# The weight ring's upper and lower tiles begin at eight offsets past a multiple of 64 bytes

## The chip, the cores and the metric

The kernel runs on one core of one Trainium2 chip. The metric is the device time of one execution in microseconds (us), as the median of several runs; the profile is one further execution, recorded by the hardware profiler. TensorE (PE) multiplies, VectorE (DVE) and ScalarE (ACT) work elementwise, GpSimd (POOL) helps, and SyncE (SP) issues the DMAs that bring the weights from HBM into SBUF, the on-chip memory of 128 partitions.

## What is computed

A trunk of two layers on 256 rows of 2,048 features. Each layer is a mixing block (retention in layer 0, mLSTM in layer 1) and an MLP, each with an RMSNorm ahead and behind. Nearly all the time goes into the products with the weights:

```python
def retention(h, w_in, w_out, cos, sin):
    q, k, v, g = split(h @ w_in)            # 2048 x 12288
    ...
    return (silu(g) * y) @ w_out            # 4096 x 2048

def mlstm(h, w_in, b_gate, norm_g, w_out):
    q, k, v, o, gates = split(h @ w_in)     # 2048 x 6160
    ...
    return (y * sigmoid(o)) @ w_out         # 2048 x 2048

def sqrelu_mlp(h, w1, w2):                  # 2048 x 8192, 8192 x 2048
    return square(relu(h @ w1)) @ w2

def reference(x, ...):
    for i in range(2):
        h = rms_norm(x, g[0])
        y = retention(h, ...) if i % 2 == 0 else mlstm(h, ...)
        x = x + rms_norm(y, g[1])
        y = sqrelu_mlp(rms_norm(x, g[2]), w1[i], w2[i])
        x = x + rms_norm(y, g[3])
    return x
```

## The kernel before

**Numbers in two parts.** TensorE multiplies in the type float32r, which keeps fewer bits than float32. So each operand is split into an upper part (rounded to float32r) and a lower part (the rest), and a product is made of three: upper by upper, upper by lower, lower by upper. The activations lie split in `hT` (all 2,048 features, upper and lower parts side by side) and in `zT` (one slice of 512).

**The ring.** The weights come in 899 loads of 128 x 1,024 float32 (`CE` = 1024 columns, 4,096 bytes in a partition). SP loads each into a tile `raw` (four of them in turn). ACT rounds `raw` into a tile `wh`, the upper part (L935), and DVE writes `wl = raw - wh`, the lower part (L954; in the first loads of a few blocks half of it falls to GpSimd, L953). `wh` and `wl` have nine tiles each (`SPLIT`), in the pool `wp`, used in turn. All tiles of a pool that have one tag lie behind each other, so that with slots of 4,096 bytes every tile of the ring has the same address modulo 64. The small tile `spare` ahead of them (224 bytes in a partition) moves the ring's start: in the built program `raw` begins at 86,720, `wh` at 103,104 and `wl` at 139,968, all multiples of 64, as `hT` (50,368) and both `zT` (176,832 and 185,024) are.

**Two forms of product.** In `mm_a` the weights stream through the array (the moving operand, 512 columns) and a 128 x 128 piece of the activations is held (the stationary operand). A load serves 12 matmuls: for each half of 128 rows of tokens, and for each of the two runs of 512 columns in the tile,

```python
nc.tensor.matmul(ps, xh, wh[:, i, cols], ...)   # L133
nc.tensor.matmul(ps, xh, wl[:, i, cols], ...)   # L134
nc.tensor.matmul(ps, xl, wh[:, i, cols], ...)   # L135
```

In `mm_b` it is the other way round: a 128 x 128 piece of the weights is held, and `hT` streams: 512 columns (upper and lower activations together) over a piece of `wh` (L145, or L148 at the end of a sum), then 256 columns (upper activations) over the same piece of `wl` (L146). A load serves eight such pairs. `mm_a` is used for v, g and o, for all products out of a block, and for the first 512 columns of each MLP; `mm_b` for q, k and the rest of the first MLP product.

**The attention's own product.** `mm_pv` (L317 to L319) has the pattern of `mm_a`: upper scores by `vh`, upper scores by `vl`, lower scores by `vh`. `vh` and `vl` are tiles of 1,032 float32, or 4,128 bytes, which is 64 times 64.5. `vh` begins at a multiple of 64; `vl`, which lies right behind, begins 32 bytes past one. In the retention layer a matmul takes 512 columns of them. In the mLSTM layer it takes 258 columns, at steps of 1,032 bytes, so that its starts are 0, 8, 16 or 24 bytes (`vh`) and 32, 40, 48 or 56 bytes (`vl`) past a multiple of 64. The scores' own tiles begin at multiples of 64.

**The order of the work** is written out by hand (`tc.manual_schedule()`): a list of steps is walked, and ahead of each step as many loads are split as the ring has room for (`gone + SPLIT`, and `pace(n)` at the start). No instruction is put elsewhere by a scheduler.

Of the kernel before, what the change touches and what calls it, by code (L numbers as in the profile page):

```python
# [10 lines left out]
F32 = mybir.dt.float32  # L11
F32R = mybir.dt.float32r
# [7 lines left out]
P = 128  # L20
# [10 lines left out]
CE = KA * 512  # L31
# [29 lines left out]
def trunk(ctx, tc, x, xt, positions, gcols, grows, w_rqk, w_rvg, w_ro, w_mqk, w_mvo, w_mg, b_gate,  # L61
# [3 lines left out]
    gap = ctx.enter_context(tc.tile_pool(name="gap", bufs=1))  # L65
    wp = ctx.enter_context(tc.tile_pool(name="wp", bufs=SPLIT))
# [5 lines left out]

    gc_sb = const.tile([P, 2, 4, KT], F32, name="gc_sb")
    nc.gpsimd.dma_start(out=gc_sb.rearrange("p a b k -> p (a b k)"), in_=gcols)
    spare = gap.tile([P, 56], F32, name="spare")
    nc.gpsimd.memset(spare, 0.0)
    ident = const.tile([P, P], F32, name="ident")
    make_identity(nc, ident)
# [42 lines left out]
    def later(delay, fn):  # L121
        due.append((now[0] + delay, fn))
# [772 lines left out]
    def pace(n):  # L895
        return (n + 1) // 2 if n < 16 else int(8 + (n - 15) * PACE)
# [9 lines left out]
    def load_to(end):  # L906
        for i in range(loaded[0], min(end, len(loads))):
            before = {1: (2, 4), 2: (4, 8), 4: (8, 12), 6: (12, 16)}
            if i in before:
                load_xt(*before[i])  # L910
            for k in range(XN * (i - X0), XN * (i - X0 + 1)):
                if 0 <= k < 8:
                    load_x(k // 4, k % 4)
            tiles[i] = wp.tile([P, CE], F32, tag="raw", name="raw", bufs=RAW)
            if i == 0:
                nc.sync.dma_start(out=tiles[i][:, 0:512], in_=w_rvg[0, 0, :, 0:512])
                load_xt(0, 2)
                nc.sync.dma_start(out=tiles[i][:, 512:CE], in_=w_rvg[0, 0, :, 512:CE])
            else:
                loads[i](tiles[i])  # L920
            loaded[0] = i + 1

    ctx.enter_context(tc.manual_schedule())
    load_to(1)
    warm_up()
    for n, (ids, fn) in enumerate(steps):
        now[0] = n
        while gone < len(loads) and last_use[gone] < n:
            gone += 1
        while split < len(loads) and split < min(gone + SPLIT, pace(n)):  # L930
            load_to(split + RAW)
            raw = tiles[split]
            wh = wp.tile([P, CE], F32R, tag="wh", name="wh")
            for part in (slice(0, 512), slice(512, CE)) if split == 0 else (slice(0, CE),):
                nc.scalar.copy(wh[:, part], raw[:, part])  # L935
            packed = split in packed_ids
            wl = wh if packed else wp.tile([P, CE], F32R, tag="wl", name="wl")
            tiles[split] = (wh, wl)

            def low_packed(wh=wh, raw=raw):  # L940
                h, r = (t.rearrange("p (t c) -> p t c", c=P) for t in (wh, raw))
                nc.vector.tensor_tensor(h[:, :, 64:104], r[:, :, 0:40], h[:, :, 0:40].bitcast(F32),
                                        op=ALU.subtract)

            def low(easy=split in easy_ids, wh=wh, wl=wl, raw=raw):
                h = wh.bitcast(F32)
                cut = CE // 2 if easy else CE
                if n == 1:
                    for part in (slice(0, 512), slice(512, CE)):
                        nc.vector.tensor_tensor(wl[:, part], raw[:, part], h[:, part], op=ALU.subtract)  # L950
                    return
                if easy:
                    nc.gpsimd.tensor_tensor(wl[:, cut:CE], raw[:, cut:CE], h[:, cut:CE], op=ALU.subtract)  # L953
                nc.vector.tensor_tensor(wl[:, 0:cut], raw[:, 0:cut], h[:, 0:cut], op=ALU.subtract)  # L954
            if packed:
                later(0, low_packed)
            elif split in ids or n < 2:
                low()
            else:
                later(0, low)  # L960
            split += 1
        fn([tiles[i] for i in ids])
        for d in [d for d in due if d[0] <= n]:
            due.remove(d)
            d[1]()
# [79 lines left out]
```

## Time and profile before

| | us |
|---|---|
| median of 3 runs | 2580.02 (2579.06 to 2583.42) |
| the profiled execution | 2580.38 |
| its span, first to last instruction | 2578.7 |
| TensorE busy | 2552.2 (99%) |
| VectorE busy | 1653.5 (64%) |
| ScalarE busy | 1199.4 (47%) |
| mean granted TensorE clock | 0.998 of full speed |

A matmul's duration in the profile is modelled and reaches past the start of the next one, since matmuls are pipelined. How fast TensorE works is therefore read from the starts: the distance from one matmul's start to the next one's. The timeline gives starts to 0.01 us, so a distance is taken over many matmuls and divided by their number.

### The profile page before, as it was taken

The numbers are of one execution on the slowest core, as the hardware profiler recorded it, in microseconds if no ns is written. First come the engines' busy times: TensorE is split into PE (matmuls) and PEld (weight loads), VectorE is DVE, ScalarE is ACT, GpSimd is POOL, SyncE is SP. The second block draws the span as 40 slices with busy tenths as digits, with TensorE's granted clock in tenths as the row PEclk, the third lists the DMA queues.
The fourth block names the chain that finished last, engine by engine and source line by source line (L and its number), as shares of the span: only waits on it lengthen the run. The fifth ranks groups of instructions, "written<-read, shape, count | busy, mean of one in ns | idle before, by whom it ended". The sixth has DMA issues, their size and how long they took to land.

```text
span 2578.7 us, 33319 instructions
## 1 busy us (share of the span) xinstructions
PE 2552.2 (99%) x12629; PEld 2152.9 (83%) x12629; DVE 1653.5 (64%) x2147; ACT 1199.4 (47%) x1602; POOL 227.0 (9%) x253
## 2 busy tenths in 40 slices
PE   8999999999999999999999999999999999999998
PEld 7888888888878888888888788888788888888887
DVE  8755665665675666656666766555866656666665
ACT  7444444444455444444444565545564444444443
POOL 1200110110130000000000210000300000000002
PEclk9999999999999999999999999999999999999999
DMA  8555555555546565655555556555465655555553
GB/s 298 195 182 195 189 171 200 184 181 182 189 141 212 186 200 175 202 184 196 181 195 180 180 191 207 176 203 186 143 218 173 197 192 191 180 199 184 189 202 124
DMA packets 135153, 486.85 MB, mean 189 GB/s; under 512 B 15368, under 2 KB 15392, under 8 KB 134992
## 3 DMA queue, kind: packets, MB, share of 16 engines
q1 hardware_dynamic: 131904, 476.11, 55.0%
q0 software_dynamic: 2512, 7.56, 1.3%
q8 instruction: 99, 1.62, 0.2%
q10 hardware_dynamic: 576, 1.05, 0.1%
q14 instruction: 62, 0.51, 0.1%
HBM read 482.55 MB, written 2.11 MB: 188 GB/s over the span
## 4 chain that ended last, share of the span: by engine, by line
PE 93%; DVE 3%; DMA 1%; issue 1%; ACT 1%; POOL 0%; DVEq 0%; ACTq 0%; POOLq 0%
PE acc L145 22%; PE acc L134 18%; PE acc L135 18%; PE acc L133 18%; PE acc L146 12%; PE acc L148 1%; DVE wl L954 1%; DMA raw<-w_mqk 1%; PE tr L397 1%; DVE hT L410 1%; DVE x_sb L358 0%; PE sc L527 0%; DMA raw<-w_mvo 0%; DVE yacc L271 0%; PE pv L319 0%
## 5 line engine op out<-in xcount | busy, mean ns | idle before, releaser
L935 ACT CAST wh<-raw 128x1024 fp32r<-128x1024 f32 (+1 forms) x899 | 936.6, 1050 | 999.7 <-PE acc L135 584.1
L954 DVE TENSOR_TENSOR wl<-raw,wh 128x1024 fp32r<-128x1024 f32 x895 | 1078.3, 1237 | 288.4 <-ACT wh L935 287.6
L145 PE MATMUL acc<-hT,wh 128*128 128x512 f32 x2520 | 894.3, 398 | 0.0
L146 PE MATMUL acc<-hT,wl 128*128 128x256 f32 x2688 | 741.3, 281 | 0.0
L145 PEld LDWEIGHTS acc<-hT,wh 128*128 128x128 f32 x2520 | 473.4, 188 | 113.7
L133 PE MATMUL acc<-wh,zT 128*128 128x512 f32 (+1 forms) x1424 | 552.2, 388 | 0.0
L135 PE MATMUL acc<-wh,zT 128*128 128x512 f32 (+1 forms) x1424 | 551.1, 387 | 0.0
L134 PE MATMUL acc<-wl,zT 128*128 128x512 f32 (+1 forms) x1424 | 550.9, 387 | 0.0
L146 PEld LDWEIGHTS acc<-hT,wl 128*128 128x128 f32 x2688 | 507.7, 189 | 7.3
L133 PE MATMUL acc<-wh,hT 128*128 128x512 f32 x828 | 326.4, 394 | 0.0
L134 PE MATMUL acc<-wl,hT 128*128 128x512 f32 x828 | 323.6, 391 | 0.4 <-DVE wl L954 0.4
L135 PE MATMUL acc<-wh,hT 128*128 128x512 f32 x828 | 323.4, 391 | 0.0
L134 PEld LDWEIGHTS acc<-wl,zT 128*128 128x128 f32 x1424 | 267.4, 188 | 54.4
L135 PEld LDWEIGHTS acc<-wh,zT 128*128 128x128 f32 x1424 | 267.3, 188 | 54.4
L133 PEld LDWEIGHTS acc<-wh,zT 128*128 128x128 f32 x1424 | 267.4, 188 | 53.1
L240 DVE TENSOR_TENSOR yacc<-acc,yacc 128x512 f32<-128x512 f32 x288 | 195.7, 690 | 164.6 <-PE acc L135 162.2
L134 PEld LDWEIGHTS acc<-wl,hT 128*128 128x128 f32 x828 | 156.1, 189 | 33.0 <-DVE wl L954 1.5
L135 PEld LDWEIGHTS acc<-wh,hT 128*128 128x128 f32 x828 | 156.0, 188 | 32.7
L133 PEld LDWEIGHTS acc<-wh,hT 128*128 128x128 f32 x828 | 156.1, 188 | 31.4
L153 DVE TENSOR_TENSOR r<-acc,r 128x256 f32<-128x256 f32 x120 | 50.5, 421 | 196.1 <-ACT r L152 196.1
L869 POOL TENSOR_TENSOR r<-r 128x512 f32<-128x512 f32 x60 | 62.5, 1041 | 1229.0 <-DVE r L867 1229.0
L872 DVE TENSOR_TENSOR zT<-r,zT 128x512 fp32r<-128x512 f32 x60 | 41.6, 693 | 73.3 <-POOL r L869 73.3
(189 smaller groups left out, 1084.3 us busy)
## 6 DMA issues: line engine op xcount, KB each, us to landing
raw<-w SPq DMA_DIRECT2D x256, 512.0 KB, 4.2
raw<-w1b SPq DMA_DIRECT2D x240, 512.0 KB, 4.5
raw<-w_rvg SPq DMA_DIRECT2D x127, 512.0 KB, 4.2
raw<-w_rqk SPq DMA_DIRECT2D x64, 512.0 KB, 4.1
raw<-w_ro SPq DMA_DIRECT2D x64, 512.0 KB, 4.2
raw<-w_mvo SPq DMA_DIRECT2D x64, 512.0 KB, 4.2
raw<-w_mqk SPq DMA_DIRECT2D x32, 512.0 KB, 4.3
raw<-w_mo SPq DMA_DIRECT2D x32, 512.0 KB, 4.3
```

Of the source, the lines that this page charges most:

```text
L133: nc.tensor.matmul(ps, xh, wh[:, i, cols], start=first and i == 0, stop=False)
L134: nc.tensor.matmul(ps, xh, wl[:, i, cols], start=False, stop=False)
L135: nc.tensor.matmul(ps, xl, wh[:, i, cols], start=False, stop=last and i == KA - 1)
L145: nc.tensor.matmul(ps[j], wh[:, i, sl], xt[:, kt0 + i, :], start=first and i == 0, stop=False)
L146: nc.tensor.matmul(ps[j][:, 0:S], wl[:, i, sl], xt[:, kt0 + i, 0:S], start=False, stop=False)
L148: nc.tensor.matmul(ps[j], wh[:, i, sl], xt[:, kt0 + i, :], start=False, stop=True)
L153: nc.vector.tensor_tensor(dst, ps[:, 0:S], dst, op=ALU.add)
L240: nc.vector.tensor_tensor(dst, box[t], dst, op=ALU.add)
L869: nc.gpsimd.tensor_tensor(r2, r, r, op=ALU.mult)
L872: nc.vector.tensor_tensor(mids[s][:, 2 * half:2 * half + 2, S:2 * S], r2, h.bitcast(F32), op=ALU.subtract)
L935: nc.scalar.copy(wh[:, part], raw[:, part])
L954: nc.vector.tensor_tensor(wl[:, 0:cut], raw[:, 0:cut], h[:, 0:cut], op=ALU.subtract)
```

## The change

The tiles of `wh` and `wl` get 16 columns more (slots of 4,160 bytes, 65 times 64, so that every slot still begins at a multiple of 64), and of each only 1,024 columns are used, which begin 2k columns, or 8k bytes, into the slot. For load number i, k is i mod 8 for `wh` and (i + i // 8) mod 8 for `wl`. So from load to load the starts go up by 8 bytes and come round after eight, and the difference between `wl` and `wh` of the same load is 8 x (i // 8 mod 8) bytes: none for eight loads, 8 bytes for the next eight, and so on. `spare` becomes 64 bytes smaller (224 to 160), which moves `raw` and the ring down by 64.

```diff
-    spare = gap.tile([P, 56], F32, name="spare")
+    spare = gap.tile([P, 40], F32, name="spare")
...
+    def shifted(k, nm):
+
+        room = wp.tile([P, CE + 16], F32R, tag=nm, name=nm)
+        return room[:, 2 * k:2 * k + CE]
+
...
-            wh = wp.tile([P, CE], F32R, tag="wh", name="wh")
+            wh = shifted(split % 8, "wh")
...
-            wl = wh if packed else wp.tile([P, CE], F32R, tag="wl", name="wl")
+            wl = wh if packed else shifted((split + split // 8) % 8, "wl")
```

Every engine's instructions stand in the same order as before, with the same shapes; only addresses differ. In the built program `raw` begins at 86,656, the slots of `wh` at 103,040 and of `wl` at 140,480; what lies behind the ring (`zT`, `vh`, `vl` and the other work tiles) moves up by 1,088 bytes, 17 times 64, and so keeps its offset past a multiple of 64; `hT` stays.

Counted over the built program, `mm_a` has 6,660 matmuls of 512 columns. In 5,424 of them the load's `wl` and `wh` have different offsets, in 1,236 the same; 820 of the 6,660 have a moving operand that begins at a multiple of 64 (before: all). `mm_b` has 2,688 pairs, with the eight offsets about equally often for either held part.

## Rows read from the trace of the kernel before

**Rows 1.** The page: span; busy time, share of span and instructions of engines.
```profile
span 2578.7 us, 33319 instructions
...
PE 2552.2 (99%) x12629; PEld 2152.9 (83%) x12629; DVE 1653.5 (64%) x2147; ACT 1199.4 (47%) x1602; POOL 227.0 (9%) x253
...
PEclk9999999999999999999999999999999999999999
```

**Rows 2.** What TensorE waited for: total us, times, longest us.
```profile
PE tr L397 <- DVE x_sb L358: 10.0, 6, 3.0
PE acc L177 <- DVE hT L581: 6.7, 1, 6.7
PE acc L134 <- DVE wl L954: 0.4, 1, 0.4
```

**Rows 3.** Groups by line and shape: count, busy us, mean ns, idle before.
```profile
L145 PE MATMUL acc<-hT,wh 128*128 128x512 f32 x2520 | 894.3, 398 | 0.0
L146 PE MATMUL acc<-hT,wl 128*128 128x256 f32 x2688 | 741.3, 281 | 0.0
L133 PE MATMUL acc<-wh,zT 128*128 128x512 f32 x1392 | 542.7, 390 | 0.0
...
L133 PE MATMUL acc<-wh,hT 128*128 128x512 f32 x828 | 326.4, 394 | 0.0
...
L148 PE MATMUL acc<-hT,wh 128*128 128x512 f32 x168 | 62.9, 396 | 0.0
```

**Rows 4.** Timeline of PE, a long run of mm_a: start us, duration, instruction.
```profile
846.65 0.39 PE L133 MATMUL acc<-wh,zT 128*128 128x512 f32 x1
...
848.26 0.39 PE L134 MATMUL acc<-wl,zT 128*128 128x512 f32 x1
...
868.21 0.39 PE L135 MATMUL acc<-wh,zT 128*128 128x512 f32 x1
```

**Rows 5.** Timeline of PE around the last retention head's mm_pv.
```profile
706.83 0.39 PE L135 MATMUL acc<-wh,zT 128*128 128x512 f32 x1
...
709.10 0.39 PE L317 MATMUL pv<-vh,pth 128*128 128x512 f32 x1
709.33 0.40 PE L318 MATMUL pv<-vl,pth 128*128 128x512 f32 x1
709.56 0.39 PE L319 MATMUL pv<-vh,ptl 128*128 128x512 f32 x1
...
711.19 0.39 PE L133 MATMUL acc<-wh,zT 128*128 128x512 f32 x1
```

**Rows 6.** Timeline of PE: mm_b under way, then where mm_b begins.
```profile
842.40 0.40 PE L145 MATMUL acc<-hT,wh 128*128 128x512 f32 x1
842.64 0.28 PE L146 MATMUL acc<-hT,wl 128*128 128x256 f32 x1
...
845.58 0.40 PE L145 MATMUL acc<-hT,wh 128*128 128x512 f32 x1
...
868.43 0.39 PE L145 MATMUL acc<-hT,wh 128*128 128x512 f32 x1
868.66 0.28 PE L146 MATMUL acc<-hT,wl 128*128 128x256 f32 x1
868.77 0.40 PE L145 MATMUL acc<-hT,wh 128*128 128x512 f32 x1
...
869.12 0.40 PE L145 MATMUL acc<-hT,wh 128*128 128x512 f32 x1
869.37 0.28 PE L146 MATMUL acc<-hT,wl 128*128 128x256 f32 x1
869.49 0.40 PE L145 MATMUL acc<-hT,wh 128*128 128x512 f32 x1
```

**Rows 7.** Timeline of PE: mm_a on 256 columns.
```profile
747.13 0.28 PE L134 MATMUL acc<-wl,zT 128*128 128x256 f32 x1
...
749.03 0.29 PE L135 MATMUL acc<-wh,zT 128*128 128x256 f32 x1
```

**Rows 8.** Timeline of PE: mLSTM's mm_pv, 18 matmuls, and the next one.
```profile
1652.86 0.28 PE L317 MATMUL pv<-vh,pth 128*128 128x258 f32 x1
...
1655.02 0.40 PE L145 MATMUL acc<-hT,wh 128*128 128x512 f32 x1
```

**Rows 9.** Groups of ACT and DVE that write the ring.
```profile
L954 DVE TENSOR_TENSOR wl<-raw,wh 128x1024 fp32r<-128x1024 f32 x883 | 1064.4, 1238 | 288.4 <-ACT wh L935 287.6
L935 ACT CAST wh<-raw 128x1024 fp32r<-128x1024 f32 x897 | 935.4, 1051 | 995.5 <-PE acc L135 584.1 <-PE acc L145 260.9 <-issue 60.2
```

## The prediction

> **What bounds the kernel now.** The page comes first: TensorE is busy for 2552.2 of the 2578.7 us of the span, at a full granted clock (2.4 GHz), and no other engine comes near (VectorE 64%, ScalarE 47%) [rows 1]. The waits say the same: TensorE waited for a part of the ring only once, for 0.4 us, and for anything else for some 17 us in all [rows 2]. So the time is the number of matmuls times the distance from one start to the next, and a change that alters neither the order nor the shapes can only act through that distance (or by slowing another engine until TensorE waits for it). The groups give the numbers [rows 3]: 2,688 pairs of `mm_b` (2,520 of L145 and 168 of L148, each with one L146), and 3 x (1,392 + 828) = 6,660 matmuls of `mm_a` with 512 columns. The timeline gives the distances. In a long run of `mm_a`, from 848.26 to 868.21 us, 88 distances take 19.95 us, or 0.2267 us each [rows 4]. In `mm_b`, nine pairs from 842.40 to 845.58 take 3.18 us, or 0.3533 us a pair [rows 6]. 6,660 x 0.2267 + 2,688 x 0.3533 = 1,510 + 950 = 2,460 us, 95% of the span: one nanosecond in the distance of `mm_a` is 6.7 us, one in the pair of `mm_b` 2.7 us.
>
> **A distance that isn't one number.** The same form of matmul doesn't always take 0.2267 us. Where `mm_a` begins after `mm_b`, its first seven distances, from 846.65 to 848.26, take 1.61 us, or 0.230 each, and only then is the pace 0.2267 [rows 4]. And `mm_pv` of the retention layer, which has the pattern of `mm_a` and the same 512 columns, is slower though it starts out of the settled pace: ten distances before it take 2.27 us (0.227 each), its first `vh` still 0.23, but the eight from the first `vl` on, 709.33 to 711.19, take 1.86 us, or 0.2325 each [rows 5]. What sets it apart from `mm_a` is that `vl` begins 32 bytes past a multiple of 64 and `vh` at one, so that the moving operand's offset changes twice in three matmuls. That is what the change brings to `mm_a`. I read the rows so: matmuls that follow each other with equal offsets fall into step and reach 0.2267; those whose offsets differ don't, and take up to 0.2325.
>
> **The change part by part.**
>
> *`mm_a` with different offsets, 5,424 of the 6,660.* The bounds: 0 if they stay in step, and 0.2325 - 0.2267 = 5.8 ns if they behave as `mm_pv`. A gain isn't excluded by arithmetic, since 512 columns at the granted 2.4 GHz are 213.3 ns and 13.4 ns are left to gain (6,660 x 13.4 = 89 us), but no stretch in the rows runs below 0.2267. The row to which they are nearest is `mm_pv`: same pattern, same number of columns. Its offsets differ by half of 64 bytes, though, and here a fifth of the 5,424 have differences as small as 8 bytes (or 56, which is 8 from the other side), and for those I expect less. So I take 4.5 ns: 5,424 x 4.5 ns = 24.4 us.
>
> *`mm_a` with equal offsets, 1,236.* Within a load nothing alternates, but from one load to the next, after 12 matmuls, the start moves by 8 bytes. If that costs one settling, as after `mm_b`, it is 7 x 3.3 ns = 23 ns a load, or 1.9 ns a matmul: 1,236 x 1.9 ns = 2.4 us. The bounds are 0 and, if they never settle, 5.8 ns, 7.2 us.
>
> *`mm_b`, 2,688 pairs.* The moving operand stays where it was; the held pieces, 128 columns of `wh` and `wl`, now begin at the eight offsets. No row shows a held operand off a multiple of 64. The bounds from the nearest rows: where `mm_b` begins out of the settled pace its first pair takes 0.34, the next 0.35, then 0.37 [rows 6]; so it has an in-step pace of its own, 0.34, that it loses after a pair. If the offsets let it keep that, the gain is 13 ns x 2,688 = 36 us; if each pair were as long as the slowest start distances near there (0.24 for the 512 columns, 0.12 for the 256), 0.36, the loss is 7 ns x 2,688 = 18 us. I take 0: the pairs are out of step already, and another offset is as likely to shorten the one distance as to lengthen the other.
>
> *Matmuls of 256 columns.* The 96 of `mm_a` on 256 columns run at 1.90 / 16 = 0.119 us with equal offsets [rows 7], and the mLSTM layer's 258 columns, with offsets from 0 to 56 bytes, at 2.16 / 18 = 0.120 [rows 8]. Short matmuls don't show a price of the offset; 0 is taken. It also says that the start's offset alone is cheap, and that it is the settled pace of the 512 that is at stake.
>
> *The writers of the ring.* ACT and DVE now write at offsets of 8k bytes, and DVE reads `wh` there. DVE has some 883 such instructions of 1.24 us and ACT 897 of 1.05 [rows 9]; DVE is idle for 925 us of the span, so each of its 883 could take 1.0 us longer before it had no time left. The cover is the ring's nine tiles and TensorE's 99%. I take 0. The loads into `raw` keep their offsets, and so do `hT`, `zT` and the work tiles.
>
> *Sum.* 24.4 + 2.4 = 26.8 us on the profiled execution's 2580.38, which is its span of 2578.7 and 1.7 around it: 2607.2. The median of the runs is 0.4 us lower, 2580.02, so 2607 there, 1.0% slower.
>
> **A rule that says otherwise.** In the rows an alternation of 0 and 32 bytes goes with 0.2325 for 0.2267 [rows 5]. The Trainium skill (SBUF — State Buffer, Specifications) states that SBUF has cachelines of 16 bytes, and that each step to a new line pays. By that rule 2,048 bytes that begin 8 bytes off a line touch 129 lines in place of 128; an estimate from the page and the row is 0.2267 / 128 = 1.8 ns for the half of the matmuls with such a start, 3,330 x 1.8 ns = 6 us, or nothing at all where the extra line is hidden. 32 bytes are two whole lines, so by it `vl` should run as `vh` does, and the trace doesn't agree.
>
> **The rivals.**
>
> *No change.* The start's offset costs nothing, and `mm_pv` is slow for another reason: its runs are only nine long, it writes to other accumulators (`psB`), and its held tiles are others. For it: the short matmuls, which run at any offset at the same pace [rows 7, 8]. Against it: `mm_pv` comes out of the settled pace, and leaves it at the very first `vl`, after a `vh` of 0.23 [rows 5]. Time: 2580, or up to 2585 where only each load's first matmuls resettle, one or two of twelve. Chance 0.14.
>
> *`mm_b` falls into step: faster.* Its pair goes from 0.3533 towards the 0.34 of its first pair [rows 6], because the held pieces no longer begin where the moving operand does. The price is up to -36 us, against +27 of `mm_a`; it decides the sign once `mm_b` keeps step for three quarters of its pairs, or for a third if `mm_a` loses only the 12 us of half the price. With all pairs in step and `mm_a` at half price: 2580 - 36 + 13 = 2557; with two thirds of the pairs: 2569. For it: the state exists in the rows. Against it: it lasts one pair there, and the eight offsets would have to serve it nearly all. Chance 0.16.
>
> *The change doesn't do what it says.* The slots' starts are multiples of 64 in the built program, and all tiles but the ring's keep their offsets, so the shifts are real. No chance is set aside.
>
> **How the numbers follow.** My forecast, `mm_a` out of step, has 0.70. Its own range runs from half the price in `mm_a` with `mm_b` unchanged, 2580 + 13 = 2593, to the full price with the loss in `mm_b`: 5,424 x 5.8 + 2.4 + 18 = 52 us, 2632. The range that is to hold 8 times in 10 takes in the rival of no change and the lesser gains in `mm_b` below it, down to 2574, and ends above at 2630; what is left out is most of the faster case and a little at the top. About 0.2%, 5 us, is what a measurement of this kernel can tell from no change. Slower by more than that: the forecast, 0.70. Within it: 0.14. Faster: 0.16.
>
> **What would show it.** In the timeline after: a long run of `mm_a` whose load has different offsets at 0.230 to 0.2325 a start, beside one with equal offsets near 0.2267; pairs of `mm_b` at 0.353; the same waits of TensorE as before. In the groups the 512-column matmuls of L133 to L135 (now some lines lower) keep their number. Wrong would be: `mm_a` at 0.2267 throughout (then the reading of `mm_pv` falls), `mm_b` at 0.34 or at 0.36 (then the held operand's offset counts, and my 0 was the error), or waits of TensorE for `wl` (then DVE pays for the offsets).

## The result and the profile after

The changed kernel takes 2605.66 us (2605.57 to 2606.89) against 2580.02: 1.0098 times as long, with an interval of 1.0075 to 1.0121. That is 25.6 us more, where 26.8 were forecast. The page of the changed kernel (span; busy time and share by engine), which answers to [rows 1]:

```profile
span 2603.9 us, 33319 instructions
...
PE 2579.9 (99%) x12629; PEld 2155.3 (83%) x12629; DVE 1652.7 (63%) x2147; ACT 1196.9 (46%) x1602; POOL 225.9 (9%) x253
```

VectorE and ScalarE are as busy as before to within 3 us, so the writers of the ring pay nothing for the offsets; the 25 us of the span are all TensorE's. What TensorE waited for (total us, times, longest us), as in [rows 2]:

```profile
PE tr L397 <- DVE x_sb L358: 7.8, 6, 2.5
PE acc L177 <- DVE hT L581: 6.4, 1, 6.4
PE acc L134 <- DVE wl L959: 0.8, 2, 0.4
```

There is no new wait. The loss is in the starts. Timeline of PE after the change, the settled part of a run of `mm_a` (its eighth to its last matmul) and the run of `mm_b` behind it, to be read as [rows 4] and [rows 6]:

```profile
904.45 0.39 PE L134 MATMUL acc<-wl,zT 128*128 128x512 f32 x1
...
924.86 0.40 PE L135 MATMUL acc<-wh,zT 128*128 128x512 f32 x1
...
926.48 0.39 PE L145 MATMUL acc<-hT,wh 128*128 128x512 f32 x1
...
943.59 0.40 PE L145 MATMUL acc<-hT,wh 128*128 128x512 f32 x1
```

The 88 distances of `mm_a` take 20.41 us, 0.2319 each (before: 0.2267), and the 49 pairs of `mm_b` take 17.11 us, 0.3492 each (before: 0.3533).

Over the whole trace, from all starts but those behind a wait (a distance of over 0.262 us): `mm_a` goes from a mean of 227.0 to 232.6 ns, and 6,602 x 5.54 ns = +36.6 us; `mm_b`'s pair from 352.7 to 349.9 ns, and 2,672 x -2.84 ns = -7.6 us. What the starts behind waits take beyond the mean distance of their kind of matmul goes from 24.1 to 21.1 us. 36.6 - 7.6 - 3.0 = 26.0, against 25.6 measured.

### The profile page after: what moved, and what is told of

The parts are those of the page before. It is cut to its first block, busy times and chain, and to the rows that moved or that the text cites. A ratio compares the mean times of both kernels' runs of the same rounds, so it can differ in the third digit from the quotient of the medians.

```text
span 2603.9 us, 33319 instructions
## 1 busy us (share of the span) xinstructions
PE 2579.9 (99%) x12629; PEld 2155.3 (83%) x12629; DVE 1652.7 (63%) x2147; ACT 1196.9 (46%) x1602; POOL 225.9 (9%) x253
## 4 chain that ended last, share of the span: by engine, by line
PE 92%; DVE 4%; DMA 1%; issue 1%; ACT 1%; POOL 1%; DVEq 0%; ACTq 0%; POOLq 0%
PE acc L145 21%; PE acc L134 19%; PE acc L133 19%; PE acc L135 19%; PE acc L146 11%; DVE wl L959 2%; PE acc L148 1%; PE tr L397 1%; DVE hT L410 1%; DMA raw<-w_mqk 1%; DVE x_sb L358 1%; PE sc L527 0%; DVE yacc L271 0%; DMA raw<-w_mvo 0%; PE pv L319 0%
## 5 line engine op out<-in xcount | busy, mean ns | idle before, releaser
L959 DVE TENSOR_TENSOR wl<-raw,wh 128x1024 fp32r<-128x1024 f32 x895 | 1078.3, 1236 | 298.0 <-ACT wh L940 296.3
L133 PE MATMUL acc<-wh,zT 128*128 128x512 f32 (+1 forms) x1424 | 560.1, 393 | 0.0
L134 PE MATMUL acc<-wl,zT 128*128 128x512 f32 (+1 forms) x1424 | 558.2, 392 | 0.0
L135 PE MATMUL acc<-wh,zT 128*128 128x512 f32 (+1 forms) x1424 | 558.0, 392 | 0.0
L133 PE MATMUL acc<-wh,hT 128*128 128x512 f32 x828 | 330.2, 399 | 0.0
L134 PE MATMUL acc<-wl,hT 128*128 128x512 f32 x828 | 327.1, 395 | 0.8 <-DVE wl L959 0.8
L135 PE MATMUL acc<-wh,hT 128*128 128x512 f32 x828 | 327.1, 395 | 0.0
L134 PEld LDWEIGHTS acc<-wl,zT 128*128 128x128 f32 x1424 | 268.7, 189 | 60.9
L135 PEld LDWEIGHTS acc<-wh,zT 128*128 128x128 f32 x1424 | 268.0, 188 | 61.5
L134 PEld LDWEIGHTS acc<-wl,hT 128*128 128x128 f32 x828 | 156.6, 189 | 36.7 <-DVE wl L959 1.6
L135 PEld LDWEIGHTS acc<-wh,hT 128*128 128x128 f32 x828 | 156.2, 189 | 36.6
```

Of the source, the lines that this page charges most:

```text
L133: nc.tensor.matmul(ps, xh, wh[:, i, cols], start=first and i == 0, stop=False)
L134: nc.tensor.matmul(ps, xh, wl[:, i, cols], start=False, stop=False)
L135: nc.tensor.matmul(ps, xl, wh[:, i, cols], start=False, stop=last and i == KA - 1)
```

## The experiments

In all of them instructions, shapes and order stay those of the kernel before, unless the diff says otherwise; only starts of tiles differ. The diffs are shortened: a value or a comment stands where the run's kernel calls a small function. Times stand beside runs of the kernel before on the same chip (2580.6 to 2581.6). "Relative start" is the start of a ring tile less that of the activations that it is multiplied with. Modulo 256 `hT` and `zT` begin alike in the kernel before and in all runs with slots of a multiple of 256 bytes. In the changed kernel and the runs built on it (slots of 4,160 bytes, the smaller `spare`) `zT`, which lies behind the ring, is 1,088 bytes further up, or 64 modulo 256, while `hT` stays.

### One constant offset, nothing alternates modulo 64

```diff
-            wh = shifted(split % 8, "wh")
+            wh = shifted(1, "wh")
...
-            wl = wh if packed else shifted((split + split // 8) % 8, "wl")
+            wl = wh if packed else shifted(1, "wl")
```

> Every tile of the ring begins 8 bytes past a multiple of 64, wh and wl of every load alike; nothing alternates and nothing moves from load to load. Theory A (the prediction's: following matmuls with different offsets fall out of step, equal ones stay in it): mm_a settles at 0.2267 us a start as before, the time is 2580 within 5 us. Theory B (a moving operand off a multiple of 64 can't keep step with held operands that are on one, whatever its neighbours): mm_a runs at 0.2325 throughout, 6,660 x 5.8 ns = +38 us, and with mm_b's pair 3 ns shorter as in the changed kernel (-8 us) some 2605 to 2612.

Measured: 2615.19 us, 1.0135 (1.0119 to 1.0150), slower than the change itself and 3 us above theory B's range. The settled part of a run of `mm_a` in its timeline (L135 and L136 are here what L134 and L135 were):

```profile
907.89 0.40 PE L135 MATMUL acc<-wl,zT 128*128 128x512 f32 x1
...
928.54 0.39 PE L136 MATMUL acc<-wh,zT 128*128 128x512 f32 x1
```

88 distances take 20.65 us, 0.2347 each. Every `wh` and `wl` is 8 bytes past a multiple of 64, and still nothing falls into step. Theory A, the prediction's own, falls in the form it was given, in offsets modulo 64. The changed kernel says it too: the mean distance in loads with equal offsets is 232.6 ns, with different ones 232.5. Modulo 256, though, the starts still move here from load to load, by the slots' 64; the case in which nothing moves at all is (8, 8) in the scan further down.

### The change in streaming loads alone, and in held loads alone

```diff
+            kh, kl = offsets(split, split in held_ids)   # (0, 0) for the other kind of load
-            wh = shifted(split % 8, "wh")
+            wh = shifted(kh, "wh")
```

> The change's offsets only in loads whose weights stream (mm_a, the moving operand); loads whose weights are held (mm_b) begin at multiples of 64. Theories A and B alike: mm_a at 0.2325, +37 us, mm_b at 0.3533 a pair as before, so 2612 to 2617, slower than the changed kernel. If the whole loss of the change came from elsewhere (the writers, the slots), this stays near 2580 or near 2606.

> The change's offsets only in loads whose weights are held (mm_b); loads whose weights stream (mm_a) begin at multiples of 64. Theories A and B alike: mm_a at 0.2267 as before; mm_b's pair 2.8 ns shorter, as the starts in the changed kernel's trace show, 2,688 x 2.8 = 7.5 us: 2572, faster than the kernel before by 0.3%. A rival: the shorter pair of the changed kernel comes from mm_a being out of step when mm_b begins; then this is 2580.

Measured: 2605.91 us (1.0099, 1.0082 to 1.0116) with the offsets in streaming loads, 2600.31 (1.0076, 1.0061 to 1.0091) with them in held loads. Both expectations missed, by 6 to 11 and by 28 us; the first run is where its text put a loss that comes from the slots or the writers ("near 2606"). The second is the telling one: all weights that stream begin at multiples of 64 there, as before the change, and yet `mm_a` in its timeline:

```profile
902.99 0.40 PE L135 MATMUL acc<-wl,zT 128*128 128x512 f32 x1
...
923.38 0.39 PE L136 MATMUL acc<-wh,zT 128*128 128x512 f32 x1
```

20.39 / 88 = 0.2317. So theory B falls as well: a multiple of 64 isn't enough. What the two kernels share with the change is the slot of 4,160 bytes, which makes the start wander by 64 from slot to slot.

### A first scan, which could not tell

> In the 28 inner slices of the two MLPs the loads have constant offsets, one pair (wh, wl) for each slice, in units of 8 bytes: (0,0), (k,k), (0,k) and (k,0) for k of 1 to 7, and six mixed ones; elsewhere mostly 0, and (0,6) in the mLSTM layer. Each slice has a run of 96 mm_a matmuls and one of 64 mm_b pairs, read from the timeline. Theory A: mm_a settles at 0.2267 in (0,0) and in all (k,k), and is at 0.230 to 0.2325 in the others. Theory B: 0.2267 in (0,0) alone, slower in (k,k) as well. For mm_b: if the held operand's offset decides, some pair is near 0.340 throughout and others near 0.353 or above; if only its changing does, all are at 0.353.

Measured, in one run: 2601.05 us, and no slice in step, not even (0,0): by their starts the slices are at 230.6 to 234.9 ns, (0,0) at 231.5. With slots of 4,160 bytes a constant offset isn't a constant start, so the slices mix nine starts each. The scan was made again below with other slots.

### The slots alone

```diff
-            wh = shifted(split % 8, "wh")
+            wh = shifted(0, "wh")
...
-            wl = wh if packed else shifted((split + split // 8) % 8, "wl")
+            wl = wh if packed else shifted(0, "wl")
```

> The changed kernel's slots of 4,160 bytes, but every tile of the ring begins at its slot's start, a multiple of 64. Theory A and B, which look at multiples of 64 alone: mm_a in step at 0.2267, 2580 within 5 us. Theory C (what must agree is the start modulo more than 64, up to the 512 bytes that a held piece is wide; the slots, which are 65 times 64 apart, break it with no offset at all): mm_a at 0.231 as in the run with offsets in the held loads alone, mm_b's pair at 0.350, 2598 to 2602.

Measured: 2598.08 us, 1.0067 (1.0052 to 1.0082). Larger slots alone, with no offset in them, cost 17.2 us, where the whole change costs 25 (what they do to the place of `zT` is part of it). `mm_a` and `mm_b` in its timeline:

```profile
901.48 0.40 PE L135 MATMUL acc<-wl,zT 128*128 128x512 f32 x1
...
921.87 0.39 PE L136 MATMUL acc<-wh,zT 128*128 128x512 f32 x1
...
923.50 0.40 PE L146 MATMUL acc<-hT,wh 128*128 128x512 f32 x1
...
940.47 0.39 PE L146 MATMUL acc<-hT,wh 128*128 128x512 f32 x1
```

20.39 / 88 = 0.2317 and 16.97 / 49 = 0.3463. Theory C stands so far.

### The offsets alone

Eight slots of 4,608 bytes take the room of nine of 4,096, and every slot begins at the same start modulo 512. Once with no offset, once with the change's:

```diff
-SPLIT = 9
+SPLIT = 8
...
+        room = wp.tile([P, CE + 128], F32R, tag=nm, name=nm)
+        return room[:, k // 4:k // 4 + CE]      # k bytes: 0, or 8 * (i % 8) and 8 * ((i + i // 8) % 8)
```

> A ring of eight slots of 4,608 bytes (nine times 512) in place of nine of 4,096, in the same room; every tile begins at its slot's start, and all tiles keep their addresses modulo 512. No offset. Control for the next run: one slot less may cost a few waits; by theory C mm_a stays at 0.2267, mm_b at 0.3533, and the time is 2580 to 2584.

> Eight slots of 4,608 bytes with the change's own offsets of 0 to 56 bytes for wh and wl: the offsets without the slots' wandering modulo 512. Theory B and the finer part of C (an offset under 64 bytes counts too): mm_a at 0.2325 and 2605 to 2615. If only the slots' distance made the loss: 2580 to 2584, as the run with no offset.

Measured: 2589.17 us without (1.0031, 1.0018 to 1.0044) and 2614.20 with the offsets (1.0127, 1.0112 to 1.0142). One slot less costs 8 us, more than expected: TensorE now waits for the lower parts,

```profile
PE acc L136 <- DVE wl L967: 6.8, 5, 2.2
```

while its distances are those of the kernel before (227.0 and 352.9 ns in the mean). The offsets cost 25.0 us on top, in the timeline of the second kernel:

```profile
950.84 0.39 PE L136 MATMUL acc<-wl,zT 128*128 128x512 f32 x1
...
971.29 0.39 PE L137 MATMUL acc<-wh,zT 128*128 128x512 f32 x1
```

20.45 / 88 = 0.2324. So either part of the change, the slots or the offsets, is enough to break the step, and the two don't add up: 17 and 25 make 25.

### The scan with slots that keep their start

> Eight slots of 4,608 bytes; in each of the 28 inner MLP slices constant offsets in bytes (wh, wl): (0,0), seven equal ones in steps of 64, equal 8, 16, 32 and 48, wh 0 with wl 64 to 448, wh 0 with wl 8, 16 and 32, wl 0 with wh 64, 128 and 256, and three mixed. hT and zT stay. Theory C: mm_a is at 0.2267 in (0,0) and where the offset is a multiple of the modulus that counts (128 or 256 if there is one below 512), near 0.231 elsewhere. If wh and wl have only to agree with each other, all equal ones are at 0.2267; if each has only to agree with the held operand, (0,256) and (256,0) show it. For mm_b some offset may give 0.340 to 0.347 throughout.

Measured, in one run: 2601.89 us. The settled parts of `mm_a` in the first six slices, relative starts 0, 64, 128, 192, 256 and 320 for `wh` and `wl` alike (timeline of PE; each pair of rows has 88 distances between them):

```profile
807.54 0.40 PE L140 MATMUL acc<-wl,zT 128*128 128x512 f32 x1
...
827.50 0.39 PE L141 MATMUL acc<-wh,zT 128*128 128x512 f32 x1
...
851.92 0.39 PE L140 MATMUL acc<-wl,zT 128*128 128x512 f32 x1
...
872.06 0.40 PE L141 MATMUL acc<-wh,zT 128*128 128x512 f32 x1
...
896.51 0.40 PE L140 MATMUL acc<-wl,zT 128*128 128x512 f32 x1
...
916.96 0.40 PE L141 MATMUL acc<-wh,zT 128*128 128x512 f32 x1
...
941.29 0.39 PE L140 MATMUL acc<-wl,zT 128*128 128x512 f32 x1
...
961.82 0.40 PE L141 MATMUL acc<-wh,zT 128*128 128x512 f32 x1
...
986.10 0.39 PE L140 MATMUL acc<-wl,zT 128*128 128x512 f32 x1
...
1006.05 0.39 PE L141 MATMUL acc<-wh,zT 128*128 128x512 f32 x1
...
1030.48 0.39 PE L140 MATMUL acc<-wl,zT 128*128 128x512 f32 x1
...
1050.62 0.40 PE L141 MATMUL acc<-wh,zT 128*128 128x512 f32 x1
```

0.2268, 0.2289, 0.2324, 0.2333, and then again 0.2267 and 0.2289: the pace comes back after 256 bytes. The slices at 384 and 448 repeat those at 128 and 192. From the starts in the same way, in ns a matmul, by relative start of (`wh`, `wl`):

| (wh, wl) | mm_a | (wh, wl) | mm_a |
|---|---|---|---|
| (0, 0), (256, 256), (0, 256), (256, 0) | 226.7 to 226.8 | (8, 8) | 232.3 |
| (64, 64) | 228.9 | (16, 16) | 231.7 |
| (128, 128) | 232.3 | (32, 32), (48, 48) | 233.3 |
| (192, 192) | 233.3 | (0, 8) | 233.3 |
| (0, 64), (0, 128), (0, 192) | 232.0, 233.3, 228.9 | (0, 16), (0, 32) | 232.0, 231.6 |

Only a relative start of 0 modulo 256 in both parts is in step; all others cost 2 to 7 ns, whether `wh` and `wl` agree or not. The same scan showed `mm_b`, by the mean of 49 pairs in each slice, between 345 and 353.2 ns a pair, and the aligned one, 353.2, was the slowest.

### Relative, or the address itself

```diff
+    pad = const.tile([P, 16], F32, name="pad")
+    nc.gpsimd.memset(pad, 0.0)
     hT = const.tile([P, KT, 2 * S], F32R, name="hT")
```

> The kernel before with 64 bytes of padding ahead of hT: hT, zT, the ring and the work tiles all move by 64 bytes together (their starts modulo 256 go from 192 to 0), with no change in how they stand to each other. If the pace depends on the moving operand's start relative to the held one's modulo 256: mm_a at 0.2267, mm_b at 0.3533, 2580 within 5 us. If it depends on the address itself: mm_a away from 0.2267, as with any other start in the scan (0.229 to 0.233), 2595 or more.

Measured: 2580.27 us beside 2580.57 for the kernel before, one run each. `mm_a` in its timeline:

```profile
936.95 0.39 PE L136 MATMUL acc<-wl,zT 128*128 128x512 f32 x1
...
956.90 0.39 PE L137 MATMUL acc<-wh,zT 128*128 128x512 f32 x1
```

19.95 / 88 = 0.2267. With all tiles moved by 64 bytes the step is kept: what counts is how the ring stands to something else that moved with it. `raw` too kept its place in the scan, so this run alone doesn't say that it is `hT` and `zT`. The run of the slots alone does. There, modulo 256, `raw` begins at 128, `zT` at 0 and `hT` at 192, and the ring's tiles at 0, 64, 128 and 192 in turn. By all its starts, loads whose two parts begin at 192 take 233.3 ns a matmul with `zT` held (130 groups of three matmuls) and 228.9 with `hT` held (58 groups), and those whose parts begin at 128, as `raw` does, take 232.7 and 233.5. The same tiles are fast or slow by the operand that is held.

### The held operand's start

> Eight slots of 4,608 bytes; in each of the 28 inner MLP slices constant offsets (wh, wl) for the loads whose weights are held, all others at 0, so that mm_a should be at 0.2267 throughout, resettled after each run of mm_b. mm_b's pair by offsets relative to hT: 0.3449 again at (64,0) and 0.3532 at (0,0), as in the last scan; if the difference of wh and wl decides, (128,64) and (192,128) are like (64,0); the others between 0.340 and 0.354. By the two scans' slots the time is 2589 less some 3 to 5 us.

Measured, in one run: 2580.19 us, 4 to 6 below the expectation, with `mm_a` at 226.7 ns in every slice (226.8 in one), and `mm_b` by relative start from 340.8 to 353.2 ns a pair. The first two slices, (64, 0) and (192, 0), with 49 pairs between each two rows:

```profile
829.12 0.39 PE L151 MATMUL acc<-hT,wh 128*128 128x512 f32 x1
...
845.82 0.39 PE L151 MATMUL acc<-hT,wh 128*128 128x512 f32 x1
...
872.74 0.39 PE L151 MATMUL acc<-hT,wh 128*128 128x512 f32 x1
...
889.43 0.39 PE L151 MATMUL acc<-hT,wh 128*128 128x512 f32 x1
```

16.70 / 49 = 0.3408 and 16.69 / 49 = 0.3406: the pace that [rows 6] show for one pair only, kept for the whole run. The difference of `wh` and `wl` alone doesn't decide ((192, 128) is at 347.6). Nor do the two starts: (64, 0) stood in the scan before as well, behind an `mm_a` that was out of step. The expectation's 0.3449 is a mean over two halves there, in the timeline of `e8_scan512`, with 28 pairs between each two rows:

```profile
2302.64 0.40 PE L151 MATMUL acc<-hT,wh 128*128 128x512 f32 x1
...
2312.53 0.40 PE L151 MATMUL acc<-hT,wh 128*128 128x512 f32 x1
...
2313.93 0.39 PE L151 MATMUL acc<-hT,wh 128*128 128x512 f32 x1
...
2323.45 0.39 PE L151 MATMUL acc<-hT,wh 128*128 128x512 f32 x1
```

9.89 / 28 = 0.3532, and, behind the end of a sum (where two pairs come in the other order), 9.52 / 28 = 0.3400. So the same starts can keep either pace, and what ran ahead decides which: the history counts too. In the scan of the held operand (192, 64) goes in the same way from 353.4 to 346.7 ns, so a mean of `mm_b` by setting can mix two paces. The kernel before, at (0, 0), has its `mm_b` at the slowest of all settings tried, 353.2.

### Versions that use it

Both put `wh` 192 bytes further in held loads alone, and leave the rest at relative start 0. That needs slots of 17 times 256 for `wh`, and the room is taken from `raw` (three tiles, nine slots) or from the ring (eight slots, and five of `raw`):

```diff
-            wh = wp.tile([P, CE], F32R, tag="wh", name="wh")
+            room = wp.tile([P, CE + 64], F32R, tag="wh", name="wh")
+            wh = room[:, 48:48 + CE] if split in held_ids else room[:, 0:CE]
```

> A version to beat both: nine slots; wh's slots have 4,352 bytes (17 times 256), and only in loads whose weights are held does wh begin 192 bytes into its slot; wl and all streaming loads stay at 0 modulo 256 relative to hT and zT. The room comes from one tile of raw less (three for four). If the relative start modulo 256 sets the pace: mm_a 0.2267, mm_b's pair 0.3408 for 0.3532, 2,688 x 12.4 ns = 33 us: 2547, plus what the shorter lead of the loads costs (0 to 10 us). If the gain is a feature of the scan's slices alone: 2580.

> The same offsets with eight slots for wh and wl and five tiles of raw. The 33 us of mm_b's step against the 8 us that eight slots cost in the control: 2554 to 2558.

Measured: 2572.58 us with three `raw` (0.9965, 0.9952 to 0.9978) and 2556.34 with eight slots (0.9902, 0.9885 to 0.9918), which beats both kernels: 25 us less than the kernel before, 49 less than the changed one. The page and the timeline of the second, a run of `mm_b` and one of `mm_a`:

```profile
span 2554.9 us, 33327 instructions
```

```profile
822.34 0.39 PE L146 MATMUL acc<-hT,wh 128*128 128x512 f32 x1
...
839.02 0.39 PE L146 MATMUL acc<-hT,wh 128*128 128x512 f32 x1
...
844.36 0.39 PE L135 MATMUL acc<-wl,zT 128*128 128x512 f32 x1
...
864.31 0.39 PE L136 MATMUL acc<-wh,zT 128*128 128x512 f32 x1
```

16.68 / 49 = 0.3404 and 19.95 / 88 = 0.2267, both in step. Over the whole trace the pairs go from a mean of 352.7 to 341.0 ns, some 31 us gained in `mm_b`; 8 are lost to the slot in its control; the profiled spans differ by 23.8. The time is in the range expected. With three `raw` the pairs are as short (340.9 ns in the mean), but the loads come late, and the time is 16 to 26 us above the expectation. The group of ACT's upper parts, whose idle time was ended almost wholly by TensorE in [rows 9], now waits for the DMA:

```profile
L939 ACT CAST wh<-raw 128x1024 fp32r<-128x1024 f32 x897 | 935.5, 1050 | 1082.6 <-DMA raw<-w1b 257.2 <-DMA raw<-w 249.7 <-PE acc L136 224.6
```

and the starts behind waits take 47.3 us beyond the mean distances, where they took 24.1. The lead of the loads was worth 23 us, and not the 0 to 10 expected.

## Why the prediction was right, and where its reason was not

**What bounds the kernel, and by what a change of addresses can act**: right. No wait came, no other engine slowed, and the sum over the starts (26.0) gives the result (25.6) to 0.4 us.

**The reading of `mm_pv`** was half right. That a start can put a run of matmuls out of step, and that this costs up to 5.8 ns, is what [rows 5] show, and the changed kernel's `mm_a` took 5.54 ns more. (In the built program `vh` begins at the same place modulo 256 as the scores' tiles that are held, and `vl` 32 bytes further: the scan's (0, 32), at 231.6 ns.) But the step that failed is the sentence "matmuls that follow each other with equal offsets fall into step". Equal offsets of 8 bytes ran at 0.2347 (0.2323 where the slots keep their start), starts all at multiples of 64 at 0.2317, and equal relative starts of 64 to 192 at 0.2289 to 0.2333. What must hold for `mm_a` is that each part's start relative to the held operand is 0 modulo 256. In the kernel before the whole ring, `hT` and `zT` met it (all start 192 past a multiple of 256), which I had not seen: the change's offsets from multiples of 64 led me to look at that alone, and I counted the larger slots as neutral since 4,160 is a multiple of 64, and the move of `zT` by 1,088 bytes as well. Together these two cost 17 us with no offset at all.

**The terms.** `mm_a` with different offsets was put at 4.5 ns, and all of `mm_a` took 5.54: 36.6 us for the 26.8 of both terms. The loads with equal offsets were put at 1.9 ns and took 5.6, as much as the others. `mm_b` was put at 0 and gained 7.6 us. Its sign was among the bounds, and the premise (out of step already) held; that another start is as likely to lengthen a pair as to shorten it did not, since in the scans no start was slower than the aligned one. So 9.8 us too little for `mm_a`, 7.6 too much for `mm_b`, and 3.0 less behind waits, which no term had: 26.8 + 9.8 - 7.6 - 3.0 = 26.0. That the forecast is near the 25.6 is luck: errors of opposite sign cancelled.

**The rivals.** That `mm_b` falls into step was given 0.16. The state does exist and can be kept, almost fully at three settings out of the 28 tried for the held operand, (192, 0), (64, 0) and (64, 240), at 340.8 to 341.7 ns, but the changed kernel's eight offsets don't keep it (349.9). No change: excluded. The Trainium skill (SBUF — State Buffer, Specifications) states that SBUF has lines of 16 bytes and that each step to a new line pays. Offsets of whole lines add no line, and by that alone they would be free; the runs don't agree: equal relative starts of 16, 64 and 192 bytes took 231.7, 228.9 and 233.3 ns for 226.7. That 8 bytes cost more than whole lines is seen in one place (0.2347 against 0.2317 with the same slots) and not in another (232.3 at 8 bytes, 233.3 at 32).

**What stays open** is the mechanism below the pace: why 256, why `mm_b` likes 192 and 64 bytes in the upper part and none (or 240) in the lower, and what lets it keep either of two paces at the same starts. That was measured, not explained. Whether an offset matters through reads of the moving operand or of the held one was not separated: only their difference was moved.

## What to carry to other kernels

When TensorE is busy throughout, read the distance between starts, not the busy share: the same matmul took 0.2267 or 0.2333 us by nothing but where its operands begin. Keep the moving and the held operands' starts equal modulo 256 bytes when weights stream as they do here (float32r, 512 columns over a held piece of 128 x 128), which includes the slot's size and everything allocated ahead of either. Try the starts one by one for other patterns, since one scan with a constant start for each slice gives the whole table; but look at the distances inside a slice too, as a mean can hide two paces. When a forecast of a sum comes true, look at the terms: here two of them were off by 10 and by 8 us with opposite signs.

## What was not expected of the hardware

- The pace of `mm_a` depends on the difference of two operands' addresses within a partition, with a period of 256 bytes: 226.7, 228.9, 232.3, 233.3 ns at 0, 64, 128 and 192 for both parts, and again from 256 on.
- It has a memory: `mm_b` at (64, 0) ran at 340.0 ns a pair behind a settled `mm_a`; behind one that was out of step it ran at 353.2 for some 30 pairs, and at 340.0 from the end of a sum on.
- An aligned start can be the worst one: `mm_b` at (0, 0) took 353.2 ns, at (192, 0) 340.8.
